# GLA in whole token groups, and the last feed-forward in token-group order: a two-layer hybrid decoder on one core

## The chip, the cores and the metric

One NeuronCore of a Trainium2 chip runs the whole step in one launch. The metric is the device time of one execution in microseconds (us). Five engines matter here: TensorE (PE in the profile, with its weight loads as PEld), VectorE (DVE), ScalarE (ACT), GpSimd (POOL) and the queue that issues DMA transfers (SP).

## The reference

A prompt of 16 learned meta tokens and 1024 tokens goes through two layers together with a sample group of 8 sequences of 4 tokens; both use the same weights. In each layer four kinds of mixers (A delta rule, B HGRN2, C GLA, D retention) work side by side on 256 columns each, then an output projection, a layer norm, a SwiGLU feed-forward and a second layer norm follow. GLA, cut to its core, is:

```python
def _gla_chunk(s, inp):
    q, k, v, g = inp                      # K = 32 per head, V = 64, 4 heads
    b = jnp.cumsum(g, axis=1)
    dec = _masked_exp(b[:, :, None] - b[:, None, :], incl)
    att = jnp.einsum('bthk,bshk,btshk->bhts', q, k, dec)
    o = einsum('bthk,bhkv->bthv', q * exp(b), s) + einsum('bhts,bshv->bthv', att, v)
    s_new = exp(b_last)[..., None] * s + einsum('bshk,bshv->bhkv', k * exp(b_last - b), v)

x = _layer_norm(ALPHA * x + m, ln1_g[l], ln1_b[l])
f = (silu(x @ w_ffn_gate[l]) * (x @ w_ffn_up[l])) @ w_ffn_down[l]
x = _layer_norm(ALPHA * x + f, ln2_g[l], ln2_b[l])
```

## The kernel before

The 1072 tokens stand in three token groups: 304 (48 leading ones and 2 blocks of 128), 384 and 384 (3 blocks of 128 each). In the last layer the meta tokens are dropped, so group 0 has 288 tokens there. Every large product is computed in three passes of single-precision halves: each operand is split into a high part (a cast on ACT) and a low part (a subtraction, mostly on DVE), and three matmuls are added up. The halves of activations and weights lie in the memory part R, of the feed-forward's hidden rows in P; other data lie in H and in P.

The program is recorded by a planner inside the kernel. Generators ("threads") yield operations; the planner keeps its own estimate of when each engine and each operand is ready and emits the operation that could start first. The order of each engine's instructions is therefore fixed when the program is built, by those estimates. One thread, main, yields the large products: the input projections, the output projection and the feed-forward (`layer_in`, `layer_out`, `layer_ffn`). Four worker threads yield the mixers' jobs, one job for a mixer and a token group; their small matmuls are put between main's large ones. Main needs every mixer's output before the output projection of the same group can end.

A GLA job works in units of token blocks. `task_units` gives group 0 a leading unit and a unit of 2 blocks, and GLA's groups 1 and 2 a unit of 2 blocks and one of 1 block (`HALVES`); the other mixers take 3 blocks at once (`UNITS`). `gated` makes a unit's attention matrix `at`, level by level (64, 32, then steps of 8, 2, 1 inside blocks of 32), for two heads at a time; `states_and_out` makes the states and the outputs; `norm_out` normalises them. All of a job's tiles lie in an arena of 3072 columns.

The feed-forward goes through 22 slices of 128 hidden rows. For a slice there is a gate and an up product for each token group, a split of their product into halves (`ffn_split`), and for each pair of slices a down product. `FFN_END` gives the order of the last nine steps. In what follows g0, u0 and d0 are the last gate, up and down step for token group 0, and so on for groups 1 and 2; a down step adds slices 20 and 21, so half of its matmuls (slice 20) do not need the gate and up just computed. After d of a group its last layer norm (`ln_group`) runs, tile by tile of 128 tokens, and each tile is written out.

The weights come one tile at a time: a transfer, a cast on ACT and a subtraction on DVE for each (`weights`, `splits`), with one buffer for the raw tile.

Of the kernel before, what the change touches and what calls it, by code (L numbers as in the profile page):

```python
# [22 lines left out]
UNITS = [[(0, 1, LEAD), (LEAD, 2, 128)], [(0, 3, 128)], [(0, 3, 128)]]  # L23
# [49 lines left out]
OUT_ORDER = [(0, range(3)), (1, range(3)), (2, [0]), (2, [1]), (3, [0]), (2, [2]), (3, [1]), (3, [2])]  # L73
FFN_END = [0, 3, 1, 4, 6, 2, 5, 7, 8]
KORD = [0, 1, 4, 5, 2, 3, 6, 7]
# [360 lines left out]
class Kern:  # L436
# [950 lines left out]
    def layer_ffn(self, l, w0):  # L1387
# [23 lines left out]
        x = order[-9:]  # L1411
        order[-9:] = [x[j] for j in FFN_END]
        for (kind, f), g in order:
# [123 lines left out]
    def gated(self, A, l, u, q, k, vs, b, es, K, first, low, upper, S, S0, bo_out, names, sf, spent):  # L1537
# [7 lines left out]
        if lead:  # L1545
            at = A.alloc(H * 48)
            yield self.zero(at)
            dst, mrows = at.r("p (h t) -> p h t", h=H), 48
        else:
            at = A.alloc(nb * H * 128)  # L1550
            yield self.zero(at)
            ac = A.alloc(nb * H * 32)
            yield self.zero(ac)
            dst, mrows = ac.r("p (h x) -> p h x", h=H), 128
        a4 = None if lead else at.r("p (h a t) -> p h a t", h=H, t=128)
        for m in list(first) if lead else list(upper) + list(low):
            wk = wq = None
# [27 lines left out]
            for j in range(H // 2):  # L1585
# [28 lines left out]
                if m == 64:  # L1614
                    yield self.copy2(a4[0:64, hs, :, 64:128], bp[0:64, :, 0:64 * nb].r("p h (a t) -> p h a t", a=nb))
                elif m == 32:
                    for z in range(2):
                        r = slice(64 * z, 64 * z + 32)
                        yield self.copy2(a4[r, hs, :, 64 * z + 32:64 * z + 64],
                                         bp[r, :, 0:32 * nb].r("p h (a t) -> p h a t", a=nb))  # L1620
# [15 lines left out]
        if not lead:  # L1636
            for z in range(4):
                r = slice(32 * z, 32 * z + 32)
                yield self.dcopy(a4[r, :, :, 32 * z:32 * z + 32], dst[r].r("p h (a t) -> p h a t", t=32))
            A.free(ac)  # L1640
        eb = A.alloc(n)
        yield self.act(AF.Exp, eb, b, scale=es)
        qe = A.alloc(n)
        yield self.tt2(qe, q, eb, MUL)
        ke = A.alloc(n)
# [7 lines left out]
        yield self.act(AF.Exp, ke, ke, scale=es)  # L1653
        yield self.tt2(ke, ke, k, MUL)
        kt = A.alloc(nb * 128)
        A.free(b)
# [6 lines left out]
        yield from self.states_and_out(A, l, u, qe, kt, vts, at, S, S0, eb, None, K, H, bo_out, names, sf)  # L1663

# [64 lines left out]

    def states_and_out(self, A, l, u, qe, kt, vts, at, S, S0, eb, gam, K, H, bo_out, names, sf):  # L1730

# [15 lines left out]
        else:  # L1747
# [4 lines left out]
            for a in range(nb):  # L1752
                sc = gam[0] if gam else eb[:, 128 * a + 127:128 * a + 128]
                yield self.stt(S[a + 1], S[a], sc,
                               bu[:, 64 * a:64 * a + 64], MUL, ADD)
# [7 lines left out]
        for j in range(nv):  # L1763
# [10 lines left out]
            for k in range(2):  # L1774
                for a in range(nb):
                    for hh in range(2):
                        h = 2 * j + hh
                        o = bo[64 * hh:64 * hh + 64, bl * a:bl * a + bl]
                        x = h * nb + a
                        if k:  # L1780
                            r = slice(K * h, K * h + K)
                            yield self.mm(o, S[a][r], qe[r, 128 * a:128 * a + 128], False, a == nb - 1)
                        else:
                            yield self.mm(o, vv(h, a), at[:, 128 * x:128 * x + 128], a == 0, False)
            if j == nv - 1:
                A.free(qe, at, *vts)
            yield from bo_out(j, bo)
# [153 lines left out]
    def ret(self, A, l, hh, g, J):  # L1941
# [24 lines left out]
        for x in self.task_units(A, J, g, self.i["sr"][l, hh]):  # L1966
# [42 lines left out]
            if u[0] + n == gn:  # L2009
                self.free(*ins)  # L2010
            yield from self.states_and_out(A, l, u, qe, kt, [vt], at, S, S0, None, gam, 64, 2, done,
                                           (None, "rs%d%d" % (l, hh)), sf)
# [646 lines left out]
```

## Time and profile before

| | before |
|---|---|
| median of 3 runs (lowest to highest) | 3121.15 us (3118.95 to 3122.83) |
| the profiled execution | 3118.43 us, its span 3116.3 us |
| mean granted TensorE clock | 0.986 of full speed |
| PE busy | 2987.8 us (96% of the span) |
| DVE busy | 1750.8 us (56%) |
| ACT busy | 1111.4 us (36%) |
| POOL busy | 391.2 us (13%) |

The span is the time from the first to the last instruction of the profiled execution. Busy time is the time in which an engine has an instruction at work; matmuls overlap each other, so a busy PE is not a PE at its peak. The granted clock is the share of full speed that the chip let TensorE have.

### The profile page before, as it was taken

The numbers are of one execution on the slowest core, as the hardware profiler recorded it, in microseconds if no ns is written. First come the engines' busy times: TensorE is split into PE (matmuls) and PEld (weight loads), VectorE is DVE, ScalarE is ACT, GpSimd is POOL, SyncE is SP. The second block draws the span as 40 slices with busy tenths as digits, with TensorE's granted clock in tenths as the row PEclk, the third lists the DMA queues.
The fourth block names the chain that finished last, engine by engine and source line by source line (L and its number), as shares of the span: only waits on it lengthen the run. The fifth ranks groups of instructions, "written<-read, shape, count | busy, mean of one in ns | idle before, by whom it ended". The sixth has DMA issues, their size and how long they took to land.

```text
span 3116.3 us, 65676 instructions
## 1 busy us (share of the span) xinstructions
PE 2987.8 (96%) x27758; PEld 2712.0 (87%) x27758; DVE 1750.8 (56%) x4142; ACT 1111.4 (36%) x2313; POOL 391.2 (13%) x444
## 2 busy tenths in 40 slices
PE   7999999999999999999999999999899999999996
PEld 5788887888999999999977888888689999999996
DVE  8877668577533333333598676684674333333336
ACT  5445667443311111111263456664342111111113
POOL 3411111000600000000033111110014000000000
PEclk9999999999999999999999999999999999999998
DMA  6311121351211111111142111124311111111112
GB/s 208 107 50 34 60 65 53 105 183 37 75 48 41 41 48 49 47 48 41 46 137 86 36 55 62 59 65 139 122 55 55 46 50 48 48 42 47 48 41 76
DMA packets 120741, 210.54 MB, mean 68 GB/s; under 512 B 32304, under 2 KB 81200, under 8 KB 120320
## 3 DMA queue, kind: packets, MB, share of 16 engines
q1 hardware_dynamic: 120448, 206.36, 20.7%
q8 instruction: 217, 3.56, 0.5%
q14 instruction: 76, 0.62, 0.1%
HBM read 162.08 MB, written 39.84 MB: 65 GB/s over the span
## 4 chain that ended last, share of the span: by engine, by line
PE 66%; DVE 7%; ACT 2%; DMA 2%; issue 1%; POOL 1%; SPq 0%; DVEq 0%; ACTq 0%; POOLq 0%
PE banks L839 64%; DVE H L870 2%; PE banks L845 1%; DVE P L870 1%; DVE H L883 1%; DVE R L870 1%; ACT H L864 1%; ACT R L861 1%; DMA H<-OF 0%; DVE H L1018 0%; POOL R L872 0%; DVE H L908 0%; DMA P<-H 0%; ACT P L864 0%; DVE P L913 0%
## 5 line engine op out<-in xcount | busy, mean ns | idle before, releaser
L839 PE MATMUL banks<-R 128*128 128x384 f32 (+3 forms) x11840 | 2091.1, 332 | 28.3 <-DVE H L883 9.4
L839 PEld LDWEIGHTS banks<-R 128*128 128x128 f32 x11840 | 1926.0, 190 | 91.3 <-issue 14.1
L870 DVE TENSOR_TENSOR H<-H,banks 128x512 f32<-128x512 f32 (+5 forms) x708 | 401.1, 570 | 522.3 <-PE banks L839 518.0
L870 DVE TENSOR_TENSOR R<-H,R 128x1024 fp32r<-128x1024 f32 (+5 forms) x376 | 358.9, 967 | 444.7 <-ACT R L861 442.0
L861 ACT CAST R<-H 128x1024 fp32r<-128x1024 f32 (+4 forms) x361 | 285.9, 806 | 817.7 <-PE banks L839 720.8
L839 PE MATMUL banks<-R,P 128*128 128x512 f32 x1584 | 371.7, 394 | 0.0
L839 PEld LDWEIGHTS banks<-R,P 128*128 128x128 f32 x1584 | 296.2, 188 | 66.7 <-issue 0.5
L864 ACT ACTIVATE H<-H 128x384 f32<-128x384 f32 (+12 forms) x477 | 204.5, 445 | 206.2 <-DVE H L1020 86.0
L872 POOL TENSOR_TENSOR H<-H 128x256 f32<-128x256 f32 (+8 forms) x206 | 194.6, 962 | 290.6 <-ACT H L864 116.1
L839 PE MATMUL banks<-H 32*32 32x32 f32 (+11 forms) x5884 | 187.2, 224 | 18.8 <-DVE H L870 6.3
L872 POOL TENSOR_TENSOR P<-H,P 128x384 fp32r<-128x384 f32 (+1 forms) x22 | 39.5, 1798 | 1274.0 <-ACT P L861 1271.7
L839 PEld LDWEIGHTS banks<-H 32*32 32x32 f32 (+6 forms) x5884 | 133.3, 120 | 75.2 <-issue 39.3
L839 PE MATMUL banks<-P 32*32 32x32 f32 (+14 forms) x6240 | 181.1, 214 | 15.7 <-DVE P L870 9.8
L839 PEld LDWEIGHTS banks<-P 32*32 32x32 f32 (+10 forms) x6240 | 132.0, 117 | 63.4 <-issue 27.5
L861 ACT COPY H<-banks 128x384 f32<-128x384 f32 (+14 forms) x313 | 115.8, 376 | 181.2 <-PE banks L839 143.3
L870 DVE TENSOR_TENSOR H<-H 128x384 f32<-128x384 f32 (+14 forms) x389 | 155.3, 417 | 43.8 <-ACT H L864 25.7
L861 ACT CAST P<-H 128x304 fp32r<-128x304 f32 (+2 forms) x132 | 64.3, 487 | 284.5 <-DVE H L870 284.5
L864 ACT ACTIVATE H<-banks 128x384 f32<-128x384 f32 (+4 forms) x166 | 70.7, 430 | 222.5 <-PE banks L839 215.5
L839 PE MATMUL banks<-P,R 128*128 128x304 f32 (+1 forms) x1056 | 147.4, 299 | 0.0
L839 PEld LDWEIGHTS banks<-P,R 128*128 128x128 f32 x1056 | 145.9, 188 | 0.0
L845 PE MATMUL banks<-H 128*128 128x128 f32 (+4 forms) x642 | 109.0, 290 | 30.3 <-DMA H<-in_cst 7.7
L845 PEld LDWEIGHTS banks<-H 128*128 128x128 f32 (+4 forms) x642 | 74.7, 142 | 62.7 <-ACT H L864 17.3
(86 smaller groups left out, 1637.9 us busy)
## 6 DMA issues: line engine op xcount, KB each, us to landing
H<-in_wst SPq DMA_DIRECT2D x208, 512.0 KB, 3.3
XR<-H SPq DMA_DIRECT2D x12, 512.0 KB, 3.4
GF<-H SPq DMA_DIRECT2D x32, 192.0 KB, 1.9
H<-XR SPq DMA_DIRECT2D x4, 1536.0 KB, 7.0
H<-XR SPq DMA_DIRECT2D x42, 128.0 KB, 2.7
XR<-H SPq DMA_DIRECT2D x42, 128.0 KB, 2.0
H<-OF SPq DMA_DIRECT2D x27, 192.0 KB, 4.6
H<-in_xin SPq DMA_DIRECT2D x8, 512.0 KB, 8.2
```

The source lines that it names most:

```text
L839: return Op("PE", cost, lambda: self.nc.tensor.matmul(out=out.x(), lhsT=lhsT.ap, rhs=rhs.ap, start=start, stop=stop), (lhsT, rhs), (out,), ...
L845: return Op("PE", 0.83 * p + 2.5, lambda: self.nc.tensor.transpose(out=out.x(), in_=in_.ap, identity=i.ap), (in_,), (out,), 20, None, tile ...
L861: fn = lambda: self.nc.scalar.copy(out=out.x(), in_=in_.x())
L864: fn = lambda: self.nc.scalar.activation(out=out.x(), in_=in_.x(), func=f, scale=s, bias=b)
L870: lambda: self.nc.vector.tensor_tensor(out=out.x(), in0=a.x(), in1=b.x(), op=op), (a, b), (out,))
L872: lambda: self.nc.gpsimd.tensor_tensor(out=out.x(), in0=a.x(), in1=b.x(), op=op), (a, b), (out,), 27.0)
L883: lambda: self.nc.vector.scalar_tensor_tensor(out=out.x(), in0=a.x(), scalar=sc, in1=b.x(), op0=op0, op1=op1),
```

## The change

GLA's groups 1 and 2 are computed in one unit of 3 blocks. To fit this in the arena, `gated` makes the steps inside the blocks of 32 first (for HGRN2 too), then allocates the attention matrix as one tile for each two heads, keeps only the last decay column of each block, and writes the transposed v over v itself, which is freed when the outputs are made. In the last layer, `FFN_END` makes the end of the feed-forward go g0 u0 d0 g1 u1 d1 g2 u2 d2.

```diff
-FFN_END = [0, 3, 1, 4, 6, 2, 5, 7, 8]
+FFN_END = [[0, 3, 1, 4, 6, 2, 5, 7, 8], [0, 3, 6, 1, 4, 7, 2, 5, 8]]
...
-        order[-9:] = [x[j] for j in FFN_END]
+        order[-9:] = [x[j] for j in FFN_END[last]]
...
-            at = A.alloc(nb * H * 128)
-            yield self.zero(at)
             ac = A.alloc(nb * H * 32)
...
-        for m in list(first) if lead else list(upper) + list(low):
+        for m in list(first) if lead else list(low) + list(upper):
+            if not lead and m == upper[0]:
+                at = [A.alloc(nb * 256) for _ in range(H // 2)]
+                for x in at:
+                    yield self.zero(x)
+                a4 = [x.r("p (h a t) -> p h a t", h=2, t=128) for x in at]
...
-                yield self.dcopy(a4[r, :, :, 32 * z:32 * z + 32], dst[r].r("p h (a t) -> p h a t", t=32))
+                for j, x in enumerate(a4):
+                    yield self.dcopy(x[r, :, :, 32 * z:32 * z + 32],
+                                     dst[r, 2 * j:2 * j + 2].r("p h (a t) -> p h a t", t=32))
...
-        qe = A.alloc(n)
-        yield self.tt2(qe, q, eb, MUL)
+        if lead:
+            qe = A.alloc(n)
+            yield self.tt2(qe, q, eb, MUL)
+        else:
+            eb, qe = A.alloc(nb), eb
+            yield self.dcopy(eb, qe.r("p (a c) -> p a c", c=128)[:, :, 127])
+            yield self.tt2(qe, q, qe, MUL)
...
-        vts = [A.alloc(nb * 128) for _ in vs]
+        place = not lead and len(vs) > 1
+        vts = vs if place else [A.alloc(nb * 128) for _ in vs]
...
-        self.free(*spent)
+        self.free(*(spent[:-len(vs)] if place else spent))
...
-        units = (HALVES if J.key[1] == "c" else UNITS)[g]
+        units = UNITS[g]
```

TensorE's order at the program's end, before. R in the sources marks large products; the rows are the twice 24 matmuls of a gate and an up step, the 48 of d0, and the 36 each of d1 and d2 (together 72); L845 are the transposes for group 0's layer norm.

```order
L839 MATMUL banks<-R 128x288 x48
L839 MATMUL banks<-R 128x384 x48
L839 MATMUL banks<-P_23748,R 128x288 x48
L839 MATMUL banks<-R 128x384 x8
L845 MATMUL banks<-H 32x128 x8
L845 MATMUL banks<-H 128x128 x8
L839 MATMUL banks<-R 128x384 x27
L845 MATMUL banks<-H 128x128 x8
L839 MATMUL banks<-R 128x384 x13
L839 MATMUL banks<-R,P_23748 128x512 x72
```

d0 stood behind g1 and u1, and d1 and d2 stood together at the end. TensorE's order at the same place, of the change:

```order
L839 MATMUL banks<-R 128x288 x48
L839 MATMUL banks<-P_23404,R 128x288 x48
L839 MATMUL banks<-R 128x384 x8
L845 MATMUL banks<-H 32x128 x8
L845 MATMUL banks<-H 128x128 x8
L839 MATMUL banks<-R 128x384 x27
L845 MATMUL banks<-H 128x128 x8
L839 MATMUL banks<-R 128x384 x13
L839 MATMUL banks<-R,P_23404 128x512 x36
L839 MATMUL banks<-R 128x384 x48
L839 MATMUL banks<-R,P_23404 128x512 x36
```

Each d step now stands straight behind its own u step, and g2 and u2 stand between d1 and d2. The first matmuls of d2 with what they wait for, of the change, on the same engine:

```order
L839 MATMUL banks<-R,P_23404 128x512 [waits DVE_49]
L839 MATMUL banks<-R,P_23404 128x512
L839 MATMUL banks<-R,P_23404 128x512 [waits Pool_49]
L839 MATMUL banks<-R,P_23404 128x512 [waits DVE_49]
L839 MATMUL banks<-R,P_23404 128x512 x2
L839 MATMUL banks<-R,P_23404 128x512 [waits Activation_49]
L839 MATMUL banks<-R,P_23404 128x512 x2
L839 MATMUL banks<-R,P_23404 128x512 [waits DVE_49]
```

Six matmuls of slice 20 stand ahead of the first one that needs slice 21's cast on ACT. VectorE's last rows before; `banks` in a source marks an addition of a d step's result, and the rows without it are layer norm (statistics, and multiplications and additions with the gain and the bias). Behind the last addition stood 39 instructions: 23 of 128x512, 7 BN_STATS, 4 BN_AGGR and 5 SCALAR_TENSOR_TENSOR; the last twelve rows of them are these:

```order
L883 SCALAR_TENSOR_TENSOR H<-H 128x1
L1020 BN_AGGR H<-H 128x2
L870 TENSOR_TENSOR H<-H 128x512
L1018 BN_STATS H<-H 128x6
L870 TENSOR_TENSOR H<-H 128x512 x2
L883 SCALAR_TENSOR_TENSOR H<-H 128x1
L1018 BN_STATS H<-H 128x6
L870 TENSOR_TENSOR H<-H 128x512
L1020 BN_AGGR H<-H 128x2
L870 TENSOR_TENSOR H<-H 128x512 x4
L883 SCALAR_TENSOR_TENSOR H<-H 128x1
L870 TENSOR_TENSOR H<-H 128x512 x6
```

Of the change, VectorE's last rows are these, all that stand behind the last addition:

```order
L1018 BN_STATS H<-H 128x6 x2
L1020 BN_AGGR H<-H 128x2
L1018 BN_STATS H<-H 128x6
L1020 BN_AGGR H<-H 128x2
L1018 BN_STATS H<-H 128x6 x2
L883 SCALAR_TENSOR_TENSOR H<-H 128x1 x2
L1020 BN_AGGR H<-H 128x2
L908 TENSOR_SCALAR H<-H 128x1024
L870 TENSOR_TENSOR H<-H 128x512 x8
L883 SCALAR_TENSOR_TENSOR H<-H 128x1
L908 TENSOR_SCALAR H<-H 128x1024
L870 TENSOR_TENSOR H<-H 128x512 x4
```

Group 1's layer norm has moved ahead of d2's additions. TensorE in the second layer's GLA, before: 32x64 makes the states (4 heads for each block), 64x128 the outputs of a unit; one unit of group 1 and one of group 2 are seen.

```order
L839 MATMUL banks<-H 32x64 x4
L839 MATMUL banks<-H 64x128 x4
L839 MATMUL banks<-P_14763 32x64 x8
L839 MATMUL banks<-R 128x384 x2
L839 MATMUL banks<-R 128x304 x4
L839 MATMUL banks<-R 128x128 x2
L839 MATMUL banks<-P_14763 64x128 x4
L839 MATMUL banks<-P_14763,H 64x128 x2
L839 MATMUL banks<-P_14763 64x128 x2
L839 MATMUL banks<-H 64x128 x4
```

Of the change, at the same place:

```order
L845 MATMUL banks<-H 128x128 x4
L839 MATMUL banks<-R 128x384 x9
L839 MATMUL banks<-H,P_14589 32x64 x8
L839 MATMUL banks<-R 128x384 x2
L839 MATMUL banks<-H 32x64 x12
L839 MATMUL banks<-P_14589,H 64x128 x6
L839 MATMUL banks<-P_14589 64x128 x2
L839 MATMUL banks<-H 64x128 x12
L839 MATMUL banks<-P_14589 48x48 x2
L839 MATMUL banks<-H 32x64 x12
L839 MATMUL banks<-R 128x256 x2
L839 MATMUL banks<-R 128x384 x7
```

The blocks of 4 and 8 have become blocks of 12, and the states of groups 1 and 2 follow each other closely. Counted over the whole built program, TensorE changes between full-array and part-array matmuls 699 times before and 665 times now, and between any two shapes of array part 884 and 832 times; it has 16 matmuls less. In the second layer 167 matmuls of large products stood between the last small matmul of the mixers and the first transpose of the first layer norm, and 202 stand there now. VectorE has 3956 instructions for 4144, ScalarE 2204 for 2315, of which ACT_TABLE_LOAD 103 for 93.

## Rows read from the trace of the kernel before

**Rows 1.** The page's first part, TensorE, VectorE and ScalarE alone.

```profile
PE 2987.8 (96%) x27758; PEld 2712.0 (87%) x27758; DVE 1750.8 (56%) x4142; ACT 1111.4 (36%) x2313; POOL 391.2 (13%) x444
```

**Rows 2.** PE by stretch: us, PE busy (count), granted clock, DMA share, GB/s.

```profile
640.00:800.00 160.00, 152.88 (x952) 0.99 0.34 111
...
2160.00:2340.00 180.00, 161.76 (x1001) 0.96 0.34 107
2340.00:3040.00 700.00, 700.00 (x4115) 1.00 0.14 47
...
3093.00:3116.00 23.00, 0.00 (x0) 0.55 0.42 160
```

**Rows 3.** PE's waits, 2160 to 2340 us: total us, times, longest.

```profile
PE banks L839 <- DVE H L883: 6.2, 2, 4.3
PE banks L839 <- ACT R L861: 4.3, 2, 4.2
PE banks L845 <- DVE H L870: 2.2, 1, 2.2
```

**Rows 4.** DMA issues, 2150 to 2240 us: count, size, median us to landing.

```profile
H<-XR SPq DMA_DIRECT2D x2, 1536.0 KB, 8.4
```

**Rows 5.** Timeline, the end on PE: start us, duration us, instructions.

```profile
3043.29 14.88 PE L839 MATMUL banks<-R 128*128 128x288 f32 x96
...
3058.01 6.56 PE L839 MATMUL banks<-P,R 128*128 128x288 f32 x48
...
3075.41 16.80 PE L839 MATMUL banks<-R,P 128*128 128x512 f32 x72
```

**Rows 6.** Timeline, the end on DVE.

```profile
3092.71 0.67 DVE L870 TENSOR_TENSOR H<-H,banks 128x512 f32<-128x512 f32 x1
...
3095.18 1.27 DVE L1018 BATCH_NORM_STATS2 H<-H 128x6 f32<-128x512 f32 x2
...
3099.58 2.47 DVE L870 TENSOR_TENSOR H<-H 128x512 f32<-128x512 f32 x4
...
3108.33 4.13 DVE L870 TENSOR_TENSOR H<-H 128x512 f32<-128x512 f32 x6
```

**Rows 7.** DVE by form, whole span: one shape: count, busy us, mean ns.

```profile
L908 DVE TENSOR_SCALAR H<-H 128x1024 f32<-128x1024 f32 x9 | 9.7, 1074 | 0.1
```

**Rows 8.** Timeline, from u1's last matmul to both halves of its hidden rows.

```profile
3058.28 0.55 DVE L870 TENSOR_TENSOR H<-H,banks 128x384 f32<-128x384 f32 x1 [5.97 <-PE banks L839]
3058.86 0.51 ACT L861 CAST P<-H 128x384 fp32r<-128x384 f32 x1 [4.29 <-DVE H L870]
...
3059.41 0.56 DVE L870 TENSOR_TENSOR P<-H,P 128x384 fp32r<-128x384 f32 x1
```

**Rows 9.** Timeline, the last weight tile's cast and subtraction.

```profile
3049.62 1.06 ACT L861 CAST R<-H 128x1024 fp32r<-128x1024 f32 x1 [2.50 <-DMA H<-in_wst]
...
3050.71 1.23 DVE L870 TENSOR_TENSOR R<-H,R 128x1024 fp32r<-128x1024 f32 x1 [0.35 <-ACT R L861]
```

**Rows 10.** PE by stretch: behind a wait of 2.00 us, and another stretch.

```profile
327.30:337.30 10.00, 9.73 (x82) 0.50 0.01 2
...
280.00:290.00 10.00, 8.97 (x139) 1.00 0.16 47
```

**Rows 11.** Timeline, PE: small blocks between large matmuls (each counted twice, two passes), and the 2.00 us wait.

```profile
327.57 0.66 PE L839 MATMUL banks<-H,P 128*128 128x64 f32 x2 [2.00 <-ACT P L861]
...
362.11 0.47 PE L839 MATMUL banks<-P 32*64 32x64 f32 x16
...
366.20 0.38 PE L839 MATMUL banks<-P 32*32 32x32 f32 x32
...
412.89 0.34 PE L839 MATMUL banks<-H 32*64 32x64 f32 x8
...
417.14 0.29 PE L839 MATMUL banks<-H 32*32 32x32 f32 x16 [0.46 <-DVE H L870]
```

**Rows 12.** The ACT table loads of the whole span: count, busy us, mean ns.

```profile
L651 ACT ACT_TABLE_LOAD x92 | 118.0, 1283 | 1.5
```

More of the change, by code (lines that the diff above doesn't have):

```diff
@@ L1554, in gated @@
             dst, mrows = ac.r("p (h x) -> p h x", h=H), 128
-        a4 = None if lead else at.r("p (h a t) -> p h a t", h=H, t=128)
-        for m in list(first) if lead else list(upper) + list(low):
+        for m in list(first) if lead else list(low) + list(upper):
[4 more added lines that the diff above has]
+                a4 = [x.r("p (h a t) -> p h a t", h=2, t=128) for x in at]
             wk = wq = None
@@ L1614, in gated @@
                 if m == 64:
-                    yield self.copy2(a4[0:64, hs, :, 64:128], bp[0:64, :, 0:64 * nb].r("p h (a t) -> p h a t", a=nb))
+                    yield self.copy2(a4[j][0:64, :, :, 64:128], bp[0:64, :, 0:64 * nb].r("p h (a t) -> p h a t", a=nb))
                 elif m == 32:
@@ L1618, in gated @@
                         r = slice(64 * z, 64 * z + 32)
-                        yield self.copy2(a4[r, hs, :, 64 * z + 32:64 * z + 64],
+                        yield self.copy2(a4[j][r, :, :, 64 * z + 32:64 * z + 64],
                                          bp[r, :, 0:32 * nb].r("p h (a t) -> p h a t", a=nb))
@@ L1654, in gated @@
         yield self.tt2(ke, ke, k, MUL)
+        A.free(b)
         kt = A.alloc(nb * 128)
-        A.free(b)
         yield from self.rows(ke, nb, bl, [lambda x: iter([self.copy2(kt[0:bl], x[0:bl, 0:nb * 128])])])
         A.free(ke)
-        vts = [A.alloc(nb * 128) for _ in vs]
+        place = not lead and len(vs) > 1
+        vts = vs if place else [A.alloc(nb * 128) for _ in vs]
         for v, vt in zip(vs, vts):
             yield from self.rows(v, nb, bl, [lambda x: iter([self.copy2(vt[0:bl], x[0:bl, 0:nb * 128])])])
-        self.free(*spent)
-        yield from self.states_and_out(A, l, u, qe, kt, vts, at, S, S0, eb, None, K, H, bo_out, names, sf)
+        self.free(*(spent[:-len(vs)] if place else spent))
+        yield from self.states_and_out(A, l, u, qe, kt, vts, at, S, S0, eb, None, K, H, bo_out, names, sf, place, spent)
     def stepped(self, A, name, q, k, b, es, n):
@@ L1728, in take_stepped, with states_and_out @@
             yield self.pred(both.r("p h a (i u) -> p h a i u", u=2)[:, :, :, :, 1], self.mk4("s1", 2, nb), src[:, :, :, 32:48])
-    def states_and_out(self, A, l, u, qe, kt, vts, at, S, S0, eb, gam, K, H, bo_out, names, sf):
+    def states_and_out(self, A, l, u, qe, kt, vts, at, S, S0, eb, gam, K, H, bo_out, names, sf, place=False, spent=()):
         c0, nb, bl = u
@@ L1752, in states_and_out @@
             for a in range(nb):
-                sc = gam[0] if gam else eb[:, 128 * a + 127:128 * a + 128]
+                sc = gam[0] if gam else eb[:, a:a + 1]
                 yield self.stt(S[a + 1], S[a], sc,
@@ L1778, in states_and_out @@
                         o = bo[64 * hh:64 * hh + 64, bl * a:bl * a + bl]
-                        x = h * nb + a
+                        x = hh * nb + a
                         if k:
@@ L1783, in states_and_out @@
                         else:
-                            yield self.mm(o, vv(h, a), at[:, 128 * x:128 * x + 128], a == 0, False)
+                            yield self.mm(o, vv(h, a), at[j][:, 128 * x:128 * x + 128], a == 0, False)
+            A.free(at[j])
             if j == nv - 1:
-                A.free(qe, at, *vts)
+                A.free(qe, *(() if place else vts))
+                if place:
+                    self.free(*spent[-len(vts):])
             yield from bo_out(j, bo)
@@ L2010, in ret @@
                 self.free(*ins)
-            yield from self.states_and_out(A, l, u, qe, kt, [vt], at, S, S0, None, gam, 64, 2, done,
+            yield from self.states_and_out(A, l, u, qe, kt, [vt], at if lead else [at], S, S0, None, gam, 64, 2, done,
                                            (None, "rs%d%d" % (l, hh)), sf)
```

## The prediction

> **What bounds the kernel now.** I read the page's first part, PE by stretch, PE's waits, and then the timeline of the end. TensorE is busy for 2987.8 of 3116.3 us while VectorE is at 56% and ScalarE at 36% [rows 1], so an edit is worth what it takes from TensorE's work, its waits, or what lies behind its last matmul. From 2340 to 3040 us it is busy for all 700 us at full clock [rows 2]: the feed-forward's large products, in which nothing is to be gained. Three other places are open. Where the mixers run, small matmuls stand between the large ones. At the end of the second layer's mixers PE is idle for 180.00 - 161.76 = 18.2 us, at a mean clock of 0.96; the same stretch of the first layer has 160.00 - 152.88 = 7.1 us at 0.99 [rows 2]. And at the end PE has stopped for the last 23 us [rows 2], while VectorE's layer norm of groups 1 and 2 runs without a gap.
>
> **The end, what it gains.** The last addition starts at 3092.71 us, and the last six multiplications and additions end at 3108.33 + 4.13 = 3112.46; less the addition's own 0.62 that is 19.1 us of VectorE behind it [rows 6]. It agrees with the count of the order: 23 of 128x512 at 2.47/4 = 0.62 make 14.3, 7 statistics at 1.27/2 = 0.63 make 4.4 [rows 6], the nine small ones what is left, 0.05 each. Now 12, 5 and 6 of these stand there, with two scalings of 1024 columns at 1.07 [rows 7], which ScalarE did before: 7.4 + 3.2 + 0.3 + 2.1 = 13.0. The tail shrinks by 6.1 us. The write of the last tile follows it in both.
>
> **The end, what it costs.** PE does the same matmuls there; it had no wait, since a d step never came straight behind its u step. Now it does, three times. From u's last matmul to the high half is some 0.15 + 0.55 + 0.05 + 0.51 = 1.2 us, and 0.5 more to the low half [rows 8]. Six matmuls of slice 20 cover it.
> - d0: g0 and u0 are 48 matmuls of 288 columns at 6.56/48 = 0.137 [rows 5], so u0 ends at 3043.29 + 6.6 = 3049.85 and the six last to 3050.7. But the last weight tile occupies ScalarE from 3049.62 to 3050.68 and VectorE from 3050.71 to 3051.94 [rows 9]; its casting is set by the raw buffer and the transfer, which the change leaves. The hidden rows' casts queue behind them: high half at 3051.15, low half at 3052.4. PE waits 0.5, does three matmuls, waits 0.8: 1.3 us.
> - d1: six of 512 columns at 16.80/72 = 0.233 [rows 5] last 1.4 us, the high half comes at 1.2: about 0.1.
> - d2: between d1's last addition and u2's multiplication VectorE has ten 128x512, four statistics and five small ones, 6.2 + 2.5 + 0.2 = 8.9 us, and 0.8 for the addition itself; PE needs only 48 x 0.165 = 7.9 us for g2 and u2 (0.165 between 0.137 for 288 and 0.233 for 512 columns). So u2's product starts at 9.7, its high half is ready at 10.8, and PE, which has work until 7.9 + 1.4 = 9.3, waits 1.5 to 2: I take 1.9, with a table load of 1.28 [rows 12] ahead of g2's Silu.
>
> Together 3.3 us; the end gains 6.1 - 3.3 = 2.8. Bounds: 6.1 with no wait, and a loss if the clock falls too (a rival).
>
> **GLA's small matmuls.** A 32x64 block of 8 passes takes 0.34 us, one of 16 takes 0.47, so 24 at once 0.60 for 0.81 apart; for 32x32, 16 take 0.29 and 32 take 0.38, so 48 take 0.47 for 0.67 [rows 11]: a block that joins another saves 0.2 us. In a group of GLA at least seven join (levels 64 and 32, the states, four of the outputs): 1.4 us, for two groups and two layers 5.6. The order bounds it otherwise: 34 changes less between full and part array are 17 excursions, 3.4 us. I take 4.5; with every block apart before (15 a group) it is 12, and below nothing it can't be, since no matmul is added. The Trainium skill, TensorEngine Tiling (Array Packing), section Key Properties, says that every change of the tiling mode drains the array. By that, all 52 changes between array shapes that go would count, at 0.2 some 10 us. The rows here don't show the changes inside an excursion apart, so I stay with the joined blocks.
>
> VectorE's 188 and ScalarE's 111 fewer instructions, the added copies and zero fills, 16 fewer transfers and ten more table loads (12.8 us at 1.28 [rows 12]) I cost at nothing: the large products cover them. Without cover the table loads alone would take back more than this term. v is held for longer, until the outputs; the order shows large products between its transposes and the outputs, so main isn't starved by that.
>
> **The end of the second layer's mixers.** The longest waits there are 4.3 us for an addition's operand (the residual, a transfer of 1.5 MB that takes 8.4 us [rows 4]), 4.2 for a cast queued on ScalarE, and 2.2 [rows 3]. Now 35 more large matmuls, 35 x 0.233 = 8.2 us, stand behind the last small one and can fill such waits. As the first layer shows, the same code can go with 11.1 us less. I take 4: half the added cover, since a wait at the head of PE's queue isn't filled by what stands behind it. Bounds: 11.1 idle and 5 of clock (0.03 x 180) at best; at worst nothing, or the second rival.
>
> **Sum.** 2.8 + 4.5 + 4 = 11.3 us off the profiled 3118.43 are 3107.1. The median of the runs shown lies 2.7 above that execution, so the forecast is 3121.15 - 11.3 = 3109.9 us. About 0.2% (6.2 us) is what a measurement can tell from no change.
>
> **Rivals.**
> - *The clock falls at the end.* After the wait of 2.00 us at 325.6 [rows 11] the clock was at 0.50, that is 1.2 GHz, for 10 us; in a stretch with 1.0 us of idle it stayed at 2.4 GHz [rows 10]. d2's wait of 1.9 is near the first. If it halves the 7 us of d2 that follow, 7 us are lost, and at d0 another 3 to 5: the end then loses 4 to 9 where it gained 2.8, and the whole is 3121.15 - 8.5 + 6.5 = 3119, no change. The Trainium skill, TensorE: Matmul & The Clock Gate, section A second HAM failure mode: psum-queue depth-cycling, speaks against this change in the same way: short idles between groups of matmuls that come often enough swing the clock between its two levels. The trace agrees that short waits can do it. For it: nothing else fills PE's queue there. Against: d0's wait is split in two. 0.20.
> - *The residual's transfers lose their cover* (the other side). One first addition has waited 4.3 us for such a transfer already [rows 3]. Four of them (two groups, two layers) stand behind mixers whose order has moved. Each uncovered costs up to 4.3 us and 5 of half clock behind it; with two more, 18 us: 3121.15 - 7.3 + 18 = 3132. It decides from 14 us on. Against it: the first layer's stretch has 7.1 us of idle in all [rows 2], and there is more cover now. 0.14.
> - *The second layer's mixers end like the first's.* 11.1 us of idle and 5 of clock go instead of 4: 3121.15 - 2.8 - 4.5 - 16 = 3098. 0.20.
> - *Joined blocks move nothing* since PE would have waited there anyway, and the layer's end stalls elsewhere: only the end's 2.8 stay, 3118. 0.06. That the change doesn't do what it says is excluded by the order.
>
> **How the numbers follow.** The forecast has 0.40, its own range 3104 to 3114. Faster by over 0.2% (below 3114.9): 0.40 and 0.20, 0.60. Within 0.2%: 0.20 and 0.06, less a little that goes on to slower, 0.24. Slower: 0.16. The range goes from 3096, just past the third rival, to 3127, short of the second: 3096 to 3127.
>
> **What would show it.** In the profile after, d0 and d2 start with a wait of about 1.3 and 2 us on PE for ScalarE or VectorE, d1 with none, and PE's last matmul is followed by 13 us of VectorE instead of 19. Blocks of 24 and 48 passes take 0.60 and 0.47 us where GLA runs. From 2160 to 2340 us PE is idle for 14 us or so. The prediction is wrong if the granted clock halves before the last matmul, if a first addition of the output projection waits for its transfer for more than 4 us, or if the stretches from 156 to 2160 us change by more than the joined blocks do.

## The result

The changed kernel takes 3088.73 us (median of 4 runs, 3087.50 to 3091.47) against 3120.05 us of the kernel before in the same comparison (3118.79 to 3122.83): a ratio of 0.990, with a 95% interval from 0.9882 to 0.9917. It is 31 us faster where 11.3 were forecast; the sign was right and the time lies outside the range of 3096 to 3127 us. The profiled execution of the changed kernel took 3087.50 us, its span is 3085.7 us, and the mean granted clock is 0.988.

The first part of its page (busy time, share of the span, instructions) answers to [rows 1]:

```profile
PE 2977.7 (96%) x27742; PEld 2710.6 (88%) x27742; DVE 1746.6 (57%) x3954; ACT 1097.8 (36%) x2202; POOL 402.0 (13%) x433
```

TensorE is busy for 10.1 us less, and its idle time inside the mixers and behind the last matmul shrinks as well. To see where, both programs are cut at equal work: at the same large matmuls of each layer, counted from the layer's start. Columns as in [rows 2]: the stretch, its length, then busy time and instructions of PE, PEld, DVE, ACT and POOL, the granted clock, the DMA share and GB/s. The kernel before:

```profile
0.00:601.40 601.40, 551.84 (x8211) 470.39 (x8212) 445.47 (x1362) 338.99 (x783) 114.85 (x171) 0.97 0.27 85
601.40:737.30 135.90, 132.43 (x911) 114.82 (x910) 89.44 (x183) 47.19 (x95) 7.21 (x7) 1.00 0.41 132
737.30:857.10 119.80, 116.15 (x683) 108.20 (x682) 76.11 (x119) 49.75 (x92) 49.80 (x35) 0.99 0.18 58
1569.30:2125.60 556.30, 527.17 (x8127) 458.63 (x8126) 413.78 (x1287) 310.50 (x727) 118.66 (x165) 0.98 0.24 74
2125.60:2279.40 153.80, 139.24 (x943) 119.99 (x943) 95.28 (x195) 51.88 (x108) 9.26 (x9) 0.96 0.37 115
2279.40:2396.50 117.10, 113.42 (x682) 105.39 (x681) 74.70 (x119) 49.23 (x92) 49.22 (x35) 1.00 0.18 59
...
3091.80:3116.30 24.50, 0.42 (x2) 0.00 (x0) 20.56 (x42) 8.08 (x13) 0.00 (x0) 0.57 0.39 150
```

The same stretches of the changed kernel:

```profile
0.00:593.90 593.90, 549.63 (x8206) 474.71 (x8207) 444.66 (x1268) 330.76 (x723) 124.32 (x167) 0.97 0.27 87
593.90:729.80 135.90, 131.94 (x909) 114.35 (x908) 89.76 (x181) 47.25 (x96) 7.15 (x8) 1.00 0.41 131
729.80:847.70 117.90, 114.39 (x680) 106.40 (x680) 76.74 (x119) 49.65 (x92) 49.86 (x35) 1.00 0.18 59
1559.90:2111.60 551.70, 525.40 (x8147) 460.89 (x8146) 411.96 (x1205) 311.62 (x689) 113.04 (x152) 0.98 0.25 75
2111.60:2254.40 142.80, 134.50 (x918) 114.69 (x917) 91.64 (x184) 45.43 (x94) 14.56 (x13) 0.99 0.39 123
2254.40:2370.70 116.30, 113.24 (x681) 105.21 (x680) 74.56 (x119) 49.35 (x92) 49.47 (x35) 1.00 0.19 60
...
2370.70:3067.50 696.80, 696.34 (x4080) 660.71 (x4080) 271.27 (x427) 127.39 (x196) 22.12 (x12) 1.00 0.14 48
3067.50:3085.70 18.20, 0.40 (x2) 0.00 (x0) 14.21 (x28) 2.45 (x7) 0.00 (x0) 0.61 0.29 115
```

The six stretches of the mixers add up to 1684.3 us before and 1658.5 after: 25.8 us less. Of these 11.0 are in one place, the end of the second layer's mixers (153.8 to 142.8 us), where PE's idle time falls from 14.6 to 8.3 us and the clock rises from 0.96 to 0.99. The first, dense stretches of both layers lose 7.5 and 4.6 us. Over all six, PE's idle time falls from 104.1 to 89.4 us, that is by 14.7, and its busy time by 11.1. The program's end gives 6.3 us of tail and takes 1.5 us in the feed-forward ahead of it (695.3 us before, all busy). The first layer's feed-forward takes 712.2 us in both.

PE's waits of the changed kernel in 2111.6 to 2254.4 us answer to [rows 3]; total us, times, longest:

```profile
PE banks L839 <- DVE H L883: 3.3, 1, 3.3
PE banks L845 <- POOL H L872: 1.8, 1, 1.8
PE banks L845 <- DVE H L870: 1.7, 1, 1.7
```

The wait of 4.2 us for a cast on ACT is gone, and of two waits for the residual's addition one of 3.3 us is left.

The end on PE, which answers to [rows 5]: d0, then d1, g2 and u2, and d2 in two rows. The last two rows are those of the weight loader in d0.

```profile
3023.82 6.83 PE L839 MATMUL banks<-P,R 128*128 128x288 f32 x48
...
3041.49 8.56 PE L839 MATMUL banks<-R,P 128*128 128x512 f32 x36
3049.89 8.54 PE L839 MATMUL banks<-R 128*128 128x384 f32 x48
3058.27 3.86 PE L839 MATMUL banks<-R,P 128*128 128x512 f32 x14
3062.50 5.40 PE L839 MATMUL banks<-R,P 128*128 128x512 f32 x22 [0.36 <-DVE P L870]
...
3023.69 2.20 PEld L839 LDWEIGHTS banks<-P,R 128*128 128x128 f32 x16
3026.10 0.96 PEld L839 LDWEIGHTS banks<-P,R 128*128 128x128 f32 x7 [0.21 <-DVE P L870]
```

d0 and d1 start without a wait. d1 runs at its old pace (3049.89 - 3041.49 = 8.40 us for 36 matmuls, 0.233 each). d0's 48 matmuls take 6.83 us where they took 6.56, so d0 lost 0.3 us; its weight loader stood once, for 0.21 us, behind sixteen loads. d2 ends at 3067.90, 9.63 us after its start, where d1's row of as many matmuls has 8.56: it lost 1.1 us. PE shows one wait of 0.36; the rest is seen on the weight loader, which stood for 0.53, 0.26 and 0.79 us:

```profile
3059.92 0.53 PEld L839 LDWEIGHTS banks<-R,P 128*128 128x128 f32 x3 [0.53 <-ACT H L864]
3060.71 0.99 PEld L839 LDWEIGHTS banks<-R,P 128*128 128x128 f32 x5 [0.26 <-DVE H L870]
3062.50 3.56 PEld L839 LDWEIGHTS banks<-R,P 128*128 128x128 f32 x16 [0.79 <-DVE P L870]
```

What these three waits end with stands on ACT and DVE:

```profile
3058.08 1.28 ACT L651 ACT_TABLE_LOAD   x1
3059.37 0.49 ACT L864 ACTIVATE H<-banks 128x384 f32<-128x384 f32 x1
...
3060.11 0.55 DVE L870 TENSOR_TENSOR H<-H,banks 128x384 f32<-128x384 f32 x1
...
3060.69 0.51 ACT L861 CAST P<-H 128x384 fp32r<-128x384 f32 x1 [0.82 <-DVE H L870]
...
3061.90 0.55 DVE L870 TENSOR_TENSOR P<-H,P 128x384 fp32r<-128x384 f32 x1
```

The first wait ends with g2's Silu (3059.86), behind a table load, and the second with u2's product (3060.66). Both end before the cast of the high half starts (3060.69), so d2's seventh and tenth matmul wait for the banks that these two instructions read, not for the hidden rows. The section on the change took the seventh's wait for ACT as that for the cast, with six matmuls of slice 20 ahead of it; twelve stand ahead of the first that needs the cast (three for each of the four banks that main has), and the high half, ready at 3061.20, holds up nothing. Only the third wait, 0.79 us, is for the hidden rows: for their low half, ready at 3062.45.

The clock stays at full speed through d2 (stretch 3058.20 to 3068.00 us):

```profile
3058.20:3068.00 9.80, 9.24 (x38) 6.41 (x36) 9.80 (x18) 4.69 (x5) 2.93 (x2) 1.00 0.44 161
```

VectorE behind the last addition, which answers to [rows 6]:

```profile
3068.44 0.67 DVE L870 TENSOR_TENSOR H<-H,banks 128x512 f32<-128x512 f32 x1
...
3072.53 0.76 DVE L908 TENSOR_SCALAR H<-H 128x1024 f32<-128x1024 f32 x1
3073.32 4.91 DVE L870 TENSOR_TENSOR H<-H 128x512 f32<-128x512 f32 x8
...
3078.33 0.81 DVE L908 TENSOR_SCALAR H<-H 128x1024 f32<-128x1024 f32 x1
3079.18 2.74 DVE L870 TENSOR_TENSOR H<-H 128x512 f32<-128x512 f32 x4
```

From the end of the last addition's 0.62 us to 3079.18 + 2.74 = 3081.92 it is 12.9 us.

### The profile page after: what moved, and what is told of

Same layout as the page of the kernel before. It is cut to its first block, busy times and chain, and to the rows that moved or that the text cites. A ratio compares the mean times of both kernels' runs of the same rounds, so it can differ in the third digit from the quotient of the medians.

```text
span 3085.7 us, 65280 instructions
## 1 busy us (share of the span) xinstructions
PE 2977.7 (96%) x27742; PEld 2710.6 (88%) x27742; DVE 1746.6 (57%) x3954; ACT 1097.8 (36%) x2202; POOL 402.0 (13%) x433
## 4 chain that ended last, share of the span: by engine, by line
PE 77%; DVE 14%; ACT 4%; DMA 2%; issue 2%; POOL 1%; SPq 0%; DVEq 0%; ACTq 0%; POOLq 0%
PE banks L839 75%; DVE H L870 3%; DVE P L870 2%; DVE H L883 2%; DVE R L870 2%; PE banks L845 2%; ACT H L864 1%; ACT R L861 1%; DMA H<-XR 1%; DVE H L908 1%; DVE H L913 1%; ACT P L864 1%; DVE H L1018 1%; ACT L651 1%; DMA H<-in_wst 1%
## 5 line engine op out<-in xcount | busy, mean ns | idle before, releaser
L870 DVE TENSOR_TENSOR R<-H,R 128x1024 fp32r<-128x1024 f32 (+3 forms) x371 | 366.2, 1001 | 440.7 <-ACT R L861 438.6
L861 ACT CAST R<-H 128x1024 fp32r<-128x1024 f32 (+3 forms) x355 | 284.0, 815 | 806.1 <-PE banks L839 721.5
L864 ACT ACTIVATE H<-H 128x384 f32<-128x384 f32 (+8 forms) x426 | 196.2, 477 | 189.6 <-DVE H L1020 90.6
L872 POOL TENSOR_TENSOR H<-H 128x256 f32<-128x256 f32 (+5 forms) x186 | 198.6, 1084 | 356.7 <-DVE H L870 137.7
L839 PE MATMUL banks<-H 32*32 32x32 f32 (+9 forms) x6192 | 189.5, 223 | 22.5 <-DVE H L870 6.9
L839 PEld LDWEIGHTS banks<-H 32*32 32x32 f32 (+5 forms) x6192 | 140.4, 119 | 74.2 <-issue 33.3
L861 ACT COPY H<-banks 128x384 f32<-128x384 f32 (+8 forms) x293 | 114.8, 398 | 209.6 <-PE banks L839 158.8
L839 PE MATMUL banks<-P 32*32 32x32 f32 (+10 forms) x5976 | 172.0, 213 | 13.2 <-DVE P L870 8.3
L839 PEld LDWEIGHTS banks<-P 32*32 32x32 f32 (+7 forms) x5976 | 126.0, 117 | 56.7 <-issue 21.4
L870 DVE TENSOR_TENSOR H<-H 128x384 f32<-128x384 f32 (+7 forms) x326 | 153.0, 490 | 22.2 <-ACT H L864 10.2
L839 PE MATMUL banks<-P,R 128*128 128x304 f32 (+1 forms) x1056 | 147.7, 299 | 0.0
L845 PE MATMUL banks<-H 128*128 128x128 f32 (+4 forms) x642 | 105.0, 285 | 28.5 <-DMA H<-in_cst 7.6
```

What stands on the lines that cost most here:

```text
L839: return Op("PE", cost, lambda: self.nc.tensor.matmul(out=out.x(), lhsT=lhsT.ap, rhs=rhs.ap, start=start, stop=stop), (lhsT, rhs), (out,), ...
L845: return Op("PE", 0.83 * p + 2.5, lambda: self.nc.tensor.transpose(out=out.x(), in_=in_.ap, identity=i.ap), (in_,), (out,), 20, None, tile ...
L861: fn = lambda: self.nc.scalar.copy(out=out.x(), in_=in_.x())
L864: fn = lambda: self.nc.scalar.activation(out=out.x(), in_=in_.x(), func=f, scale=s, bias=b)
L870: lambda: self.nc.vector.tensor_tensor(out=out.x(), in0=a.x(), in1=b.x(), op=op), (a, b), (out,))
L872: lambda: self.nc.gpsimd.tensor_tensor(out=out.x(), in0=a.x(), in1=b.x(), op=op), (a, b), (out,), 27.0)
```

## The experiments

The theory after the result: the end is worth 4 to 5 us, the joined blocks some 8, and the rest comes from PE's idle time and clock, which hang on how the planner's order happens to fall. The main rival: whole groups take these waits away by themselves.

**The parts alone.** One kernel is the change without the new end:

```diff
-        order[-9:] = [x[j] for j in FFN_END[last]]
+        order[-9:] = [x[j] for j in FFN_END[0]]
```

The other is the kernel before with the new end (and its new table `FFN_END`) only:

```diff
-        order[-9:] = [x[j] for j in FFN_END]
+        order[-9:] = [x[j] for j in FFN_END[last]]
```

> The GLA part alone, with the old order of the last feed-forward. The trace after puts 25.6 us of the gain of 30.6 us into the two mixer stretches (9.4 in the first layer, 16.4 in the second) and 4.7 into the end. If the two parts add up, this kernel is 26 us faster than before (3094). If the end's order mattered for the mixers too, or the other way round, it is not: a rival in which the parts are entangled gives anything from 3089 to 3121.

> The new order of the last feed-forward alone. By the trace after: 6.2 us less behind the last matmul and 1.5 us of waits, so 4.7 us faster (3115.5). By the prediction's own terms 2.8 us (3117). If the waits halve the clock there, no gain.

The kernel before had 3119.26 us there. GLA alone: 3094.69 us, ratio 0.9927 (0.9907 to 0.9946), as expected if the parts add up. The end alone: 3116.40 us, ratio 0.9991 (0.9980 to 1.0002), which the times by themselves don't tell from nothing; the stretches do. The last feed-forward and the tail with the end alone:

```profile
2395.80:3093.00 697.20, 696.53 (x4082) 660.77 (x4080) 271.41 (x427) 127.29 (x196) 22.11 (x12) 1.00 0.15 48
3093.00:3111.20 18.20, 0.38 (x2) 0.00 (x0) 14.24 (x28) 2.45 (x7) 0.00 (x0) 0.63 0.29 115
```

And with GLA alone, where both are as before:

```profile
2372.20:3067.60 695.40, 695.40 (x4080) 660.85 (x4080) 263.62 (x412) 122.07 (x190) 20.45 (x11) 1.00 0.14 45
3067.60:3092.00 24.40, 0.45 (x2) 0.01 (x1) 20.48 (x42) 8.08 (x13) 0.00 (x0) 0.55 0.39 150
```

695.3 + 24.5 = 719.8 us with the old end and 715.4 or 715.0 with the new one: 4.4 to 4.8 us, in both kernels. By the times the parts are 24.6 and 2.9 us, 27.4 together, against 31.3 for the whole in a comparison of its own; by the stretches, 24.3 us of mixers (1684.3 to 1660.0) and 4.4 of the end, against 25.8 and 4.8. TensorE's order in the mixers is the same with and without the new end, so these executions also show an unchanged order twice: 1684.3 and 1683.6 us before, 1658.5 and 1660.0 us with the change. Two executions can lie further apart: over 16 of the kernel before in one of the comparisons below, the whole time goes from 3111.28 to 3129.08 us. A difference of 25 us between medians is not that scatter.

**Does GLA's gain need whole groups?** Two kernels have the rewritten `gated` and the old end. The first uses halves in both layers:

```diff
-        units = UNITS[g]
+        units = (HALVES if J.key[1] == "c" else UNITS)[g]
```

The second uses them in the second layer only:

```diff
-        units = UNITS[g]
+        units = (HALVES if J.key[1] == "c" and J.key[0] else UNITS)[g]
```

> GLA rewritten as in the change (inner steps first, split attention tiles, v in place) but still in units of 2 and 1 blocks, with the old end. Theory 1: the gain comes from joining the units, so this is within 6 us of before (3115 to 3126). Rival: the gain comes from the new order of the mixers' small matmuls that the planner makes after any such edit; then this kernel moves by 10 us or more, either way.

> As e3_halves, but whole groups in the first layer alone. Theory 1: it gains what the first layer's stretch gained in the trace after, 9 us against e3_halves, and the second layer's stretch is that of e3_halves. Rival (order by chance): the two layers' stretches move by amounts that have nothing to do with which layer has whole groups.

Halves in both layers: 3138.67 us, ratio 1.0065 (1.0050 to 1.0081), slower than before. In this order the rewriting alone brings nothing. Halves in the second layer only: 3096.12 us, ratio 0.9936 (0.9921 to 0.9951), as fast as whole groups in both with the same old end (3094.69). Theory 1 fell in both: the first kernel is not within 6 us of before, and between the two the first layer's mixers differ by 18.0 us where it had 9, and the second layer's, with the same units, by 19.8 where it had nothing. The rival, order by chance, fits both. The second layer's dense stretch and the end of its mixers, halves in both:

```profile
1580.40:2150.20 569.80, 535.18 (x8161) 464.79 (x8160) 422.97 (x1342) 312.72 (x735) 110.85 (x168) 0.97 0.24 73
2150.20:2294.90 144.70, 135.83 (x911) 116.89 (x909) 92.68 (x183) 46.05 (x95) 7.16 (x7) 0.96 0.39 123
```

With halves in the second layer only:

```profile
1562.50:2120.80 558.30, 530.81 (x8161) 460.42 (x8160) 422.77 (x1332) 316.19 (x741) 118.91 (x172) 0.99 0.25 75
2120.80:2257.30 136.50, 132.45 (x910) 114.48 (x909) 89.92 (x182) 47.47 (x97) 4.27 (x6) 0.99 0.41 130
```

Both compute the same units there, with 9072 and 9071 matmuls in these two stretches, and one needs 714.5 us, the other 694.8, as little as whole groups (694.5). The difference is idle time (43.5 and 31.5 us) and the clock. So a fast second layer does not need whole groups; but one draw does not tell what is usual. In the first layer the halves' end of the mixers had one wait of 5.2 us for VectorE (total us, times, longest):

```profile
PE banks L845 <- DVE H L870: 5.2, 1, 5.2
```

**Draws of the order.** The planner has two numbers for changing the array's shape: in its estimates the first puts off a small matmul that would follow a large one, the second a large one that would follow a small one. They change which operation comes next and no computation (27758 matmuls before and 27742 after at every setting). They were moved a little in the kernel before and in the changed kernel alike, so that each setting is one draw: one order out of many that the planner could as well have made. There are six pairs, at 590, 610, 620, 580 and 640 of the first number and at 160 of the second:

```diff
-HOLD, SLACK = 600.0, 150.0
+HOLD, SLACK = 590.0, 150.0
```

> The kernel before with one number of the planner at 590 instead of 600 (a due time that is only put off), so that the same instructions stand in another order. Theory (the part of the gain that is not the joined blocks and not the end comes from how the order happens to fall: waits at the end of a layer's mixers): the small matmuls between large ones cost as before (443 to 445 us for both layers) but the two mixer stretches, 857 and 827 us before, each move by up to 15 us either way, so the time is anywhere from 3100 to 3140 us, and moves with PE's idle time and the half-clock time. Rival (whole groups take these waits away): no halves, no change, the time stays within 6 us of 3120 us. Second rival (the order of before was an unlucky one): 10 to 20 us faster than before.

> The changed kernel with the planner's number at 590. Theory: the small matmuls cost 434 to 436 us as in the changed kernel, the end keeps its 13 us behind the last addition, but the mixer stretches (848 and 811 us) move by up to 15 us each, so the time is anywhere from 3075 to 3110 us; the mean of the two perturbed changed kernels lies some 13 us (9 of blocks, 4 to 5 of the end) under that of the two perturbed kernels before. Rival (whole groups take the waits away): within 6 us of 3089 us, and 30 under the perturbed kernels before. Second rival (order of before unlucky, that of the changed kernel not): near 3089 us while those of before come down to 3105 us.

> As the one at 590, with the number at 610. Theory: 3100 to 3140 us with the small matmuls' cost unchanged at 443 to 445 us. Rival: within 6 us of 3120 us. Second rival: 3100 to 3110 us.

> As the changed kernel at 590, with 610. Theory: 3075 to 3110 us. Rivals: within 6 us of 3089 us.

> The kernel before with the planner's first number at 620: one more draw of the order. From the nine mixer parts so far (both layers' mixers together) a sum fits within 3 us: 1566 us, less 7 in whole groups, plus PE's idle time in them, plus a third of the half-clock time. Theory (blocks and end are sure, the rest is the draw): this sum holds within 5 us with no 7 us off, and the time is 3100 to 3135 us. Rival (whole groups also take idle and half-clock time away as a rule): the same sum, but over all pairs of before and changed at equal numbers the changed one has less idle and half-clock time each time.

> The changed kernel at 620. Theory: the sum 1566 - 7 + idle + a third of the half-clock time holds within 5 us, the time is 3080 to 3115 us, and idle and half-clock time may be more or less than those of before at 620. Rival: both less than at 620 before, by some 10 and 18 us, and the time 20 us under it.

> The kernel before with the planner's second number at 160 instead of 150: another draw. Theory: the sum within 5 us, 3100 to 3135 us. Rival: more idle and half-clock time than the changed kernel at 160.

> The changed kernel with the second number at 160. Theory: the sum with 7 us off holds within 5 us, 3080 to 3115 us, idle and half-clock time on either side of those of before at 160. Rival: both less, the time 20 us under before at 160.

> The kernel before with the planner's first number at 580, a further draw. So far the pairs at 600, 590, 610, 620 and at 160 of the second number have the changed kernel faster by 31, 20, 11, 22 and 26 us, with 14.5, 2.9, 1.1, 2.9 and 1.5 us less idle time of PE in the mixers. Theory (blocks 7, end 4 to 5, the rest a draw): the pair at 580 may differ by anything from 0 to 30 us, and idle time and half-clock time go either way. Rival (whole groups take idle and half-clock time away as a rule): the changed kernel has less of both and is 15 to 30 us faster.

> The changed kernel at 580; what each theory expects of the pair stands with the kernel before at 580.

> The kernel before at 640. Theory: 3095 to 3140 us, and the pair differs by 0 to 30 us, idle and half-clock time either way. Rival: more idle and half-clock time than the changed kernel at 640, 15 to 30 us slower than it.

> The changed kernel at 640; what each theory expects of the pair stands with the kernel before at 640.

Each cell has the kernel before and the changed one. Times are medians; the rest is from the profiled execution: length and PE's idle time of both layers' mixers (from the layer's first instruction to its first down matmul), and half-clock time, the sum of the records there with a granted clock of 0.50 (1.2 GHz).

| numbers | time, us | difference | mixers, us | PE idle, us | half clock, us |
|---|---|---|---|---|---|
| 600, 150 | 3120.05, 3088.73 | 31.3 | 1684.3, 1658.5 | 96.3, 81.8 | 68, 58 |
| 590 | 3125.99, 3106.51 | 19.5 | 1705.2, 1685.9 | 96.4, 93.5 | 126, 92 |
| 610 | 3100.79, 3089.50 | 11.3 | 1666.4, 1657.0 | 80.5, 79.4 | 51, 58 |
| 620 | 3114.86, 3092.80 | 22.1 | 1682.0, 1661.2 | 88.6, 85.7 | 68, 68 |
| 600, 160 | 3119.30, 3093.17 | 26.1 | 1680.2, 1664.1 | 88.6, 87.1 | 72, 65 |
| 580 | 3107.59, 3089.01 | 18.6 | 1673.4, 1661.7 | 84.9, 88.3 | 75, 65 |
| 640 | 3121.15, 3094.83 | 26.3 | 1684.6, 1662.9 | 92.9, 86.8 | 82, 55 |
| mean | 3115.7, 3093.5 | 22.2 | 1682.3, 1664.5 | 89.8, 86.1 | 78, 66 |

Idle time leaves out the 7 to 8 us ahead of the first matmul, which the stretches above contain. Length, idle time and half-clock time come from one execution of each kernel, so they hold the scatter between executions too; those profiled at 590 are the slowest of their kernels, 13 and 8 us above the medians. The draw is large: the kernel before moves over 25 us by a number that changes no computation. Its two extremes, first and second layer, at 590 and then at 610:

```profile
0.00:869.00 869.00, 811.94 (x9800) 706.14 (x9801) 610.60 (x1650) 433.86 (x974) 178.52 (x218) 0.96 0.28 88
1581.20:2417.40 836.20, 789.19 (x9749) 691.28 (x9748) 583.88 (x1593) 411.80 (x930) 179.98 (x214) 0.97 0.26 79
```

```profile
0.00:847.10 847.10, 799.96 (x9799) 692.68 (x9800) 613.34 (x1650) 436.79 (x969) 181.26 (x227) 0.99 0.28 90
1559.30:2378.60 819.30, 778.11 (x9749) 682.44 (x9748) 584.96 (x1603) 413.01 (x929) 182.82 (x207) 0.98 0.26 81
```

And the change is worth something in every pair: 22.2 us on the mean, with a standard deviation of 6.5 over the seven, so 16 to 28 us at 95%. Outside the mixers the seven profiled pairs differ by 4.5 to 5.2 us (the spans' difference less the mixers'), which is the end again. A least-squares fit over the 14 mixer lengths gives 1566 us, plus the idle time, plus 0.34 us for each us at half clock, less 10.2 us in whole groups, and misses none by more than 5.2 us (the standard errors are 0.05 on the 0.34 and 1.8 on the 10.2). The two kernels with halves, which the fit did not use, bear it out. With halves in both layers (104.0 us of idle time, 89 at half clock) and nothing off it gives 1700.3 us, and 1699.4 were measured: the rewriting itself costs and gains nothing that shows, and that kernel's 15 us over the kernel before are idle time and clock. With whole groups in one layer (84.2 and 38 us) and half of the 10.2 off it gives 1658.1, and 1661.6 were measured. By the fit the mean gain of the mixers, 17.8 us, is 10.2 of work, 3.7 of idle time and 0.34 x 11.7 = 3.9 of clock. In the pair that was to be forecast, 25.8 us are 14.5 of idle time, 0.34 x 10 = 3.5 of clock and, as the rest, 7.8 of work.

What follows: the end's gain and the work come back in every draw, and the fit prices the work on this kernel. Idle time is mostly a draw: 14.5 us less in the pair 600, 150, 1.1 to 6.1 less in five, 3.4 more at 580. Of the expectation that the sum holds within 5 us, three of the four kernels at 620 and 160 kept it; the changed kernel at 620 was 6.3 us under it. Every time lies in the range that the theory gave it, but these ranges are 30 to 45 us wide, and the first layer's mixers of the changed kernel at 590 moved by 18 us where it had 15 at most; its separate figures for the small matmuls' cost (443 to 445 and 434 to 436 us) are left open. The rival that whole groups take idle and half-clock time away as a rule had less of both in every pair; it is so in four of the seven (not at 610, 620 and 580). The strict rival, by which halves wait and whole groups don't, fell: the times at 610 before (3100.79) and at 590 changed (3106.51) are 19 and 18 us from where it had them (the changed kernel at 590 has 93.5 us of idle time and 92 us at half clock, more than the kernel before at 610). So did the second rival, that only the order of before was unlucky: at 590 the kernel before was 6 us slower still, and the changed one 18 us slower. That whole groups take away some 8 us of idle time and clock together on the mean is likely, but not settled by seven pairs. No draw beats the changed kernel by more than the runs scatter; at 610 it has 3089.50 us.

## Why the prediction was wrong

**The end, what it gains (6.1): right.** 12.9 us of VectorE stand behind the last addition where 13.0 were counted, and the tail shrank by 6.3 us (24.5 to 18.2). The sum came out better than its terms: the two scalings took 0.76 and 0.81 us, not 1.07 each, and the other rows with the gaps between them made up the difference.

**The end, what it costs (3.3): 1.5, and the cover was miscounted.** I let six matmuls of slice 20 stand ahead of the first that needs the hidden rows' high half. More stand there, and the high half delayed nothing. d1's 0.1 was right (no wait). d2 lost 1.1 us instead of 1.9: its weight loads waited 0.53 us for g2's Silu and 0.26 for u2's product, whose banks they needed, and 0.79 for the low half. That these 1.6 us come near my 1.9 is in part luck; what was right is that the table load and VectorE's layer norm hold up g2 and u2. d0 lost 0.3 instead of 1.3: sixteen loads, not nine, went ahead of the one that waits for the low half, and the last weight tile's cast started 1.0 us ahead of d0 where I had 0.2. With the end alone that cast started just ahead of d0 (3048.91 against 3048.95 us), and d0 took 3051.64 + 4.56 - 3048.95 = 7.25 us, 0.7 more than before:

```profile
3048.95 2.47 PE L839 MATMUL banks<-P,R 128*128 128x288 f32 x16
3051.64 4.56 PE L839 MATMUL banks<-P,R 128*128 128x288 f32 x32 [0.23 <-DVE P L870]
```

The end gained 4.4 to 4.8 us, not 2.8.

**The clock's fall at the end: did not come.** PE's longest idle there is 0.36 us, and the clock stays at 1.00 (2.4 GHz). The warning that short idles between groups of matmuls, where they come often enough, swing the clock (the Trainium skill, TensorE: Matmul & The Clock Gate, section A second HAM failure mode: psum-queue depth-cycling) is neither borne out nor refuted by so short an idle.

**GLA's small matmuls (4.5): too small.** By the fit the work fell by 7.8 us in this pair and by 10.2 on the mean, inside the bounds of 0 to 12. A block's own row was even slower than I extrapolated: 24 passes of 32x64 take 0.74 us and 48 of 32x32 take 0.62, not 0.60 and 0.47.

```profile
1859.32 0.62 PE L839 MATMUL banks<-H 32*32 32x32 f32 x48
...
1875.44 0.74 PE L839 MATMUL banks<-H 32*64 32x64 f32 x24
```

What I left out is the time around a block. Call it an excursion when PE leaves the large matmuls for small ones and comes back. Taken from the last large matmul's start to the next one's start, less that matmul's own time, the traces have at full clock and without idle 0.47 us for 16 of 32x32, 0.48 for 32, and 0.64 for 48 (medians of 15, 38 and 76 places in six of these traces): joining gives 0.31 us, not 0.2. And there were more excursions to lose: in the mixers 430 before and 410 after in this pair, and 426 to 440 against 395 to 408 in the other six, where I counted 17 fewer. 29 fewer on the mean at 0.31 are 9 us, and 16 large matmuls fewer a further 0.9 (16 of 256 columns, 0.12 us each from start to start, and 16 of 128, as long, became 16 of 384, 0.175 us each); the 20 of this pair and the same 0.9 are 7.1, against 7.8. This is an estimate: the 0.31 is that of 32x32 blocks alone. The Trainium skill, TensorEngine Tiling (Array Packing), section Key Properties, says that a change of the tiling mode drains the array. With 0.2 us for every change the prediction had some 10 us by it, which is nearer to the measured sum than mine. No run here shows the drain or its price apart, so this agreement may be chance.

**The end of the second layer's mixers (4): the step that failed for this pair.** It gained 11.0 us, 6.3 of them idle time. Most of the rest is the clock: the half-clock records there add up to 13.7 us before, each beginning in a wait of 1.8 to 4.3 us or at most 1.6 us behind one, and to 3.4 us after, behind the wait of 3.3. The forecast filled waits with more large matmuls; what happened is that the order was drawn anew, and the cast's wait of 4.2 us did not come again. The third rival, that this place goes like the first layer's (3098 us, given 0.20), came nearest. Yet it is no rule either: at the same two cuts this stretch has 153.8, 135.6, 160.3, 139.8, 136.6, 147.7 and 141.8 us in the seven kernels before (at 600, 580, 590, 610, 620 and 640 and with 160; mean 145.1) and 142.8, 140.5, 146.5, 141.7, 144.5, 149.2 and 140.9 in the seven changed (mean 143.7): on the mean the change brings 1.4 us here. The kernel before stood at a poor draw, the second longest of the fourteen, and the change drew again. That this place would get better was a fair guess from its twin in the first layer; that the added cover does it is not what the seven pairs show, and the size of 11 us was the draw's.

**The stretches from 156 to 2160 us, costed by the joined blocks alone: also wrong.** The dense stretches lost 7.5 and 4.6 us in this pair, and the first layer's last stretch 1.9. No idle time or clock was counted for them, though the two dense stretches gave 8.1 of the 14.7 us of idle time (49.6 to 44.3 and 29.1 to 26.3 us).

**The residual's transfers and the other edits: as forecast.** PE waits for no first addition in that stretch longer than 3.3 us. The added copies and zero fills show no loss of their own: the kernel with halves in both layers has them, and the fit needs no term for it.

The sum by the prediction's own steps: 4.7 instead of 2.8 at the end; 7.8 instead of 4.5 of work; 18 of idle time and clock instead of 4, of which about 8 are what the seven pairs have on the mean and 10 came with this draw.

## What to carry to other kernels

Where a planner or scheduler sets the order, an edit in one place draws all later waits anew. Perturb such a number that computes nothing, in the old and the new kernel alike, before a difference of less than 1% is put down to the edit: here it was 31 us in one pair and 11 to 31 over seven. A stretch that waits unusually long compared with its twin in another layer may get better by any reordering: here the 153.8 us became shorter in five of six draws that change no computation, and longer in one.

Price a small block of matmuls between large ones by the time from large to large, not by the block's own row.

## What the runs showed of the hardware that was not expected

A us at half clock cost only a third of a us where the mixers run (the fit's 0.34, with a standard error of 0.05), not half; why is not shown. And a wait of the weight loader of 1.6 us in three pieces cost PE 1.1 us, while PE's own rows show 0.36 us of idle time: the busy time of matmul rows hid most of the loss, and only the step's length against the same matmuls elsewhere showed it.
